# A decoder block's expert stage: which 128 tokens gather their experts, when, and which operand of the up product is stationary

## The chip, the cores and the metric

One core of one Trainium2 chip runs the whole layer in one launch. Its engines run their own instruction streams: TensorE (PE; weight loads PEld), VectorE (DVE), ScalarE (ACT), GpSimd (POOL) and SyncE (SP, used for DMA issue). The metric is the device time of one execution in microseconds; lower is better.

## The reference, cut to what matters

```python
h = rmsnorm(x, norm1_g);  z = h @ w_in                      # 512 tokens x 2048
a_out = chunked_spatial_gating(gelu(zu), gelu(zv), ...)
b_out = sliding_window_attention(zq, zk, zvv, sinks)
x = x + concatenate([a_out, b_out]) @ w_out
h2 = rmsnorm(x, norm2_g)
# peer(h2): 8 heads, 128 x 128 product keys, 16 experts of 16384 for each head and token
q = h2 @ w_query;  s1, s2 = q @ sub_keys
experts, gates = top16(top16(s1) + top16(s2)), softmax
a = gelu(h2 . expert_down[experts]);  x = x + sum(gates * a * expert_up[experts])
out = rmsnorm(x, norm_f_g)
```

## The kernel before

The 512 tokens are four blocks of 128. Every product is made of three matmuls in fp32r (`mm3`, L131 to L133): high part by high part, high by low, low by high. The weights come as chunks of 1 MiB (`wraw`, two buffers), loaded by SP in the order of use (L100). Each chunk is two pieces of 1024 columns; a piece is split by ACT into its high part (`whi`, L110) and by DVE or POOL into the rest (`wlo`, L112), into four buffers, two pieces ahead of PE. The load of chunk n+2 can start when both pieces of chunk n are split. `W.on_pool` is the list of pieces whose `wlo` POOL makes; from the thirteenth down chunk on it is always DVE.

The program is one long sequence:

- **A**, 26 chunks: norm, input projection, attention, spatial gating.
- **B**, 16 chunks: output projection of all four blocks (`project`, 512 columns of weights moving, the mixer's tokens `mxh`, `mxl` stationary; 24 matmuls for a piece), residual, second norm, turn to columns (`to_columns`).
- **C**, 16 chunks: queries. Blocks 0 to 2 ("dense") have the tokens moving, 384 columns; block 3 ("gathered", `GB`) has the weights moving. Behind each quarter come the scores, and `choose`, which is VectorE work (`best16`), is put into a `Filler` that a call `fill.tick(budget)` empties between matmuls.
- **D**, 51 down chunks: `dn` = 128 experts by 384 tokens, 48 matmuls, gelu, stored in `a_dram`. Between them run what is left of the choice, the decoding of it (`decode`), and a table of gates: 96 `quad`s of four tokens, each with one-hot rows `eq` (DVE, L719) and `p1` (DVE L726 or ACT), a product `p2` on POOL (L722), four matmuls of 256 columns (L738), and an evacuation by ACT (`low`) and DVE (`stage`, L754).
- **E and F**: 77 more down chunks and 128 up chunks. `up` has the dense tokens stationary and 512 columns of weights moving, three blocks, 4608 matmuls in all; each quarter is added by DVE to the tokens' rows `acc` (L978). Block 3 never meets the dense products: for each of its tokens 128 experts' rows (down, then up) are fetched by indirect DMA in halves of 1024 columns (`fetch`, L879, 512 of them, issued by POOL) and consumed by one VectorE instruction each (`unit`, L894 and L901), against `half_row` in PSUM. They are paced over this part alone.
- The last quarter of the last `up` runs block by block, with the final norm and the output behind each.

## Time and profile before

| | us |
|---|---|
| median of 3 runs (range) | 3049.59 (3042.21 to 3051.31) |
| profiled execution, span | 3046.2 |
| stage A, 0 to 388.9 | 388.9 |
| stage B, 388.9 to 582.0 | 193.1 |
| stage C, 582.0 to 786.5 | 204.5 |
| stage D, 786.5 to 1339.0 | 552.5 |
| stages E and F, 1339.0 to 3035.0 | 1696.0 |
| tail, 3035.0 to 3046.2 | 11.2 |

The profile gives no more of the profiled execution than its span; that lies inside the range of the runs, 3.4 us under their median. The stages are cut by hand at the first or last matmul of each. A row of the view of busy time by stretch has the stretch, its length, the busy time of PE, PEld, DVE, ACT and POOL with their instruction counts, the granted TensorE clock (1.00 is full), the busy share of the DMA engines and GB/s. In a timeline a row is start, length, engine, line, operation, output and input tile, form, count, and in brackets the idle time before it and what ended it. Matmuls overlap, so their spacing is read from their starts, not from their lengths. In a group of instructions the numbers behind the count are busy time, mean ns of one, and idle time of the engine just before them.

### The profile page before, as it was taken

What the parts mean: (1) busy time and instruction counts of PE and PEld (TensorE: products, weight loads), DVE (VectorE), ACT (ScalarE), POOL (GpSimd) and SP (SyncE); (2) the same over time, 40 slices, a digit from 0 to 9 for tenths busy, and PEclk for the clock granted to TensorE, in tenths of its full rate; (3) what the DMA queues carried; (4) which work ended last, traced back from release to release, by engine and by line L of the source; (5) the groups of instructions that cost most, each with busy time, mean ns of one, the idle gap of its engine ahead of it and who ended that gap; (6) DMA issues with size and microseconds to landing.
All of it is one profiled execution on the core that took longest, in us unless ns stands there. A gap on an engine that the chain in (4) does not pass through costs nothing.

```text
span 3046.2 us, 38888 instructions
## 1 busy us (share of the span) xinstructions
PE 2939.4 (96%) x15021; PEld 2623.7 (86%) x15021; DVE 2228.9 (73%) x3266; ACT 1095.9 (36%) x1699; POOL 1220.4 (40%) x754
## 2 busy tenths in 40 slices
PE   7999999999989888999999999999999999999998
PEld 6888878799989888898788889898998989899896
DVE  3125642359998999967888887878888888888864
ACT  3244432222236655643323233232322323232333
POOL 2132100334435555633344344545445454554522
PEclk9999999999999999999999999999999999999999
DMA  5221242322334444569888888998989898898953
GB/s 188 90 82 57 70 166 88 120 83 84 110 115 159 155 168 160 195 250 350 302 312 333 328 304 316 328 328 311 331 312 339 312 336 314 318 340 314 338 212 132
DMA packets 193866, 696.85 MB, mean 229 GB/s; under 512 B 16528, under 2 KB 81296, under 8 KB 148240
## 3 DMA queue, kind: packets, MB, share of 16 engines
q1 hardware_dynamic: 104960, 378.04, 35.0%
q0 software_dynamic: 73728, 268.47, 24.4%
q10 hardware_dynamic: 14992, 47.86, 4.0%
q8 instruction: 118, 1.93, 0.3%
q14 instruction: 68, 0.56, 0.1%
HBM read 650.78 MB, written 43.52 MB: 228 GB/s over the span
## 4 chain that ended last, share of the span: by engine, by line
PE 49%; DVE 20%; issue 15%; POOL 10%; ACT 3%; DMA 2%; ACTq 0%; POOLq 0%; SPq 0%; DVEq 0%
POOL row L879 10%; PE dn L133 5%; PE acc L131 5%; PE dn L132 5%; PE dn L131 5%; PE acc L133 5%; PE acc L132 5%; PE up L132 5%; PE up L131 5%; PE up L133 5%; DVE wlo L112 4%; DVE stage L754 3%; DVE eq L719 2%; DVE cand L572 1%; PE tr L339 1%
## 5 line engine op out<-in xcount | busy, mean ns | idle before, releaser
L110 ACT CAST whi<-wraw 128x1024 fp32r<-128x1024 f32 x628 | 639.7, 1048 | 738.9 <-DMA wraw<-in_up 321.1
L112 DVE TENSOR_TENSOR wlo<-wraw,whi 128x1024 fp32r<-128x1024 f32 x550 | 719.5, 1312 | 252.9 <-ACT whi L110 251.9
L133 PE MATMUL dn<-h2d,wlo 128*128 128x384 f32 x2048 | 695.2, 339 | 28.8 <-DVE wlo L112 25.6
L131 PE MATMUL dn<-h2d,whi 128*128 128x384 f32 x2048 | 694.0, 339 | 8.4 <-ACT whi L110 8.4
L132 PE MATMUL dn<-h2d,whi 128*128 128x384 f32 x2048 | 692.3, 338 | 0.0
L131 PE MATMUL up<-whi,gah 128*128 128x512 f32 x1536 | 598.9, 390 | 3.2 <-DVE acc L978 3.0
L132 PE MATMUL up<-wlo,gah 128*128 128x512 f32 x1536 | 598.8, 390 | 3.0 <-DVE wlo L112 3.0
L133 PE MATMUL up<-whi,gal 128*128 128x512 f32 x1536 | 598.3, 390 | 0.0
L879 POOL DMA_INDIRECT row<-in_down_rows,idx x256 | 367.6, 1436 | 492.0 <-DVE row L894 470.2
L879 POOL DMA_INDIRECT row<-in_up_rows,idx x256 | 364.7, 1425 | 366.4 <-DVE half_row L901 345.5
L133 PEld LDWEIGHTS dn<-h2d,wlo 128*128 128x128 f32 x2048 | 388.1, 190 | 37.3 <-DVE wlo L112 33.1
L112 POOL TENSOR_TENSOR wlo<-wraw,whi 128x1024 fp32r<-128x1024 f32 x78 | 194.9, 2519 | 559.0 <-ACT whi L110 559.0
L131 PEld LDWEIGHTS dn<-h2d,whi 128*128 128x128 f32 x2048 | 388.5, 190 | 10.5 <-ACT whi L110 10.1
L132 PEld LDWEIGHTS dn<-h2d,whi 128*128 128x128 f32 x2048 | 388.4, 190 | 0.4
L131 PEld LDWEIGHTS up<-whi,gah 128*128 128x128 f32 x1536 | 288.8, 188 | 65.9 <-DVE acc L978 4.7
L132 PEld LDWEIGHTS up<-wlo,gah 128*128 128x128 f32 x1536 | 288.6, 188 | 63.3 <-DVE wlo L112 4.4
L133 PEld LDWEIGHTS up<-whi,gal 128*128 128x128 f32 x1536 | 288.8, 188 | 60.0
L901 DVE SCALAR_TENSOR_TENSOR half_row<-row,wgt,half_row 128x1024 f32<-128x1024 f32 x256 | 328.9, 1285 | 14.8 <-DMA row<-in_up_rows,idx 11.7
L894 DVE SCALAR_TENSOR_TENSOR row<-row,half_row 128x1024 f32<-128x1024 f32 x256 | 307.1, 1215 | 18.9 <-DMA row<-in_down_rows,idx 17.3
L722 POOL TENSOR_TENSOR p<-eq,gT 128x1024 fp32r<-128x1024 bf16 x96 | 236.2, 2468 | 206.9 <-DVE eq L719 196.0
L978 DVE TENSOR_TENSOR acc<-up,acc 128x512 f32<-128x512 f32 x192 | 129.3, 690 | 92.5 <-PE up L133 92.3
L951 ACT ACTIVATE aa<-dn 128x384 f32<-128x384 f32 x72 | 35.4, 492 | 348.2 <-PE dn L133 348.2
(194 smaller groups left out, 3441.6 us busy)
## 6 DMA issues: line engine op xcount, KB each, us to landing
wraw<-in_down SPq DMA_DIRECT2D x128, 1024.0 KB
wraw<-in_up SPq DMA_DIRECT2D x128, 1024.0 KB
wraw<-in_win SPq DMA_DIRECT2D x26, 1024.0 KB
g_dram<-stage ACTq DMA_DIRECT2D x24, 1024.0 KB
g<-g_dram SPq DMA_DIRECT2D x32, 768.0 KB
wraw<-in_wout SPq DMA_DIRECT2D x16, 1024.0 KB
wraw<-in_wq SPq DMA_DIRECT2D x16, 1024.0 KB
aa<-a_dram SPq DMA_DIRECT2D x56, 192.0 KB
```

Of the source, the lines that this page charges most:

```text
L110: self.nc.scalar.copy(hi, src)
L112: eng.tensor_sub(lo, src, hi.bitcast(F32))
L131: nc.tensor.matmul(ps, wh, xh, start=start, stop=False)
L132: nc.tensor.matmul(ps, wh, xl, start=False, stop=False)
L133: nc.tensor.matmul(ps, wl, xh, start=False, stop=stop)
L719: nc.vector.tensor_tensor(eq, iota[:, None, :].to_broadcast([P, 4, P]), t[:, 1, four, None].to_broadcast([P, 4, P]), op=OP.is_equal)
L722: nc.gpsimd.tensor_tensor(p2, eq[:, :, None, :].to_broadcast([P, 4, 2, P]), hl[:, four, :, None].to_broadcast([P, 4, 2, P]), op=OP.mult)
L754: nc.vector.tensor_tensor(stage[h][:, :, o:o + 4], ps[:, :, 0, k].rearrange("p t k -> p k t"), low[:, :, k].rearrange("p t k -> p k t"), o ...
L879: nc.gpsimd.indirect_dma_start(out=t, out_offset=None, in_=src, in_offset=bass.IndirectOffsetOnAxis(ap=idx[:, j, h:h + 1], axis=0))
L894: nc.vector.scalar_tensor_tensor(t, t, 1.0, half, op0=OP.mult, op1=OP.mult, accum_out=dots[:, j, h:h + 1])
L901: nc.vector.scalar_tensor_tensor(half, t, wgt[:, j:j + 1], half, op0=OP.mult, op1=OP.add)
L978: nc.vector.tensor_add(y, ps[b], y)
```

## The change

Block 0 takes the place of block 3 as the gathered block, and its part is done first. After the mixer, block 0 alone runs through the output projection (16 chunks), two chunks of the others' projection, and its queries (16 chunks); then the others' projection (14 chunks) and queries (16). `w_out` and `w_query` are so loaded and split twice: 32 chunks more. The gathered work of block 0 (512 units) is queued as soon as its choice is decoded, and is now issued from `mm3` by a rate (`Flow`) from the others' projection on. The last 32 tokens of block 3 leave the dense products too (`EX`), so these have 352 columns in place of 384: their 128 experts each are gathered as 4 groups of 32 on the 128 partitions, 128 units more. `up` has the weights stationary and the 352 tokens moving, 6144 matmuls, and adds into `accT` (columns); at the end the result is turned back to rows (`rows_out`). POOL makes a third to three quarters of the `wlo` in every stage after A. In the tables the two parts of a gate are added in PSUM by a second matmul, and the evacuation is ACT's alone; 88 quads. `half_row` has its PSUM from the output projection on.

```diff
-    chunks += [a["wout"][i] for i in range(16)]
-    chunks += [a["wq"][i] for i in range(16)]
+    chunks = [a["win"][i] for i in range(26)] + wout + wout[:2] + wq + wout[2:] + wq
...
-    W.on_pool = [range(0, 4), range(20, 36), range(2 * 42 - 2, 2 * 70)]
+    LEAD, REST, ASK, EXPERTS = 52, 52 + 68, 52 + 96, 52 + 128
+    def on_pool(p):
+        if p < LEAD:
+            return p < 4 or 20 <= p < 36
+        if p < REST:
+            return p % 3 == 2
+        if p < ASK:
+            return p % 2 == 0
+        if p < EXPERTS + 2 * OPEN:
+            return p % 4 != 0 if p < EXPERTS else p % 2 == 0
+        return p % 3 == 0
...
+class Flow:
+    def step(self, ns):
+        if not self.q:
+            return
+        self.credit = min(self.credit + ns * self.rate, 3.0)
+        while self.q and self.credit >= 1.0:
+            self.credit -= 1.0
+            self.q.popleft()()
...
     def mm3(ps, w, x, start, stop):
...
+        flow.step(3 * ps.shape[-1] * COL_NS)
...
+    for q in range(4):
+        ps = acc_tile()
+        for i in range(8):
+            project(ps, 0, i, W.get())
+        residual(ps, 0, q)
...
+    for g in range(4):
+        ps = row_tile()
+        for i in range(8):
+            hi, lo = W.get()
+            for k in range(2):
...
+                mm3(ps, (hT0[0][:, kt, :], hT0[1][:, kt, :]), (hi[:, c], lo[:, c]),
+                    kt == 0, kt == KT - 1)
+            if soon and i % 2:
+                soon.popleft()()
+            fill.tick(2.0)
...
+        residual(ps[b - 1], b, 3)
+        dst = second_norm(b)
+        turned = (dst, h2d, (b - 1) * P)
...
+    to_columns(*turned)
...
                 def products():
-                    ps = pst2.tile([P, 4, 2, P], F32, name="tr", bufs=3)
+                    ps = pst2.tile([P, 4, P], F32, name="tr", bufs=4)
                     for j in range(4):
-                        nc.tensor.matmul(ps[:, j].rearrange("p a k -> p (a k)"), p1[:, j, :],
-                                         p2[:, j].rearrange("p a k -> p (a k)"),
-                                         start=True, stop=True)
+                        for i in range(2):
+                            nc.tensor.matmul(ps[:, j], p1[:, j, :], p2[:, j, i, :],
+                                             start=i == 0, stop=i == 1)
...
-                    nc.scalar.copy(low, ps[:, :, 1, :])
...
-                        nc.vector.tensor_tensor(stage[h][:, :, o:o + 4],
...
+                        nc.scalar.copy(stage[h][:, :, o:o + 4],
+                                       ps[:, :, k].rearrange("p t k -> p k t"))
...
-            fill.tick(2.7)
+        fill.tick(2.4)
...
+            ps = [late["ps"].tile([P, TD], F32, name="up", bufs=4) for _ in range(4)]
+            def multiply(m, j, w):
+                k = (j % 2) * 512 + m * P
+                x = ga[CB * c + j]
+                mm3(ps[m], (w[0][:, k:k + P], w[1][:, k:k + P]), x, j == 0, j == CB - 1)
...
+            w = [W.get(1), W.get(2)]
+            for m in range(4):
+                for j in range(4, 8):
+                    multiply(m, j, w[j // 2 - 2])
+                y = accT[:, 4 * q + m, :]
...
+                    nc.vector.tensor_add(y, ps[m], y)
...
+    def rows_out(q):
+        for b in range(ND):
...
+            for m in range(4):
+                nc.tensor.transpose(ps[:n, m * P:(m + 1) * P],
+                                    late["acc"][:, 4 * q + m, b * P:b * P + n], ident)
+            y = late["x"][b]
+            nc.vector.tensor_add(y[:n, cols], ps[:n], y[:n, cols])
+            square(b, n, y, q, nc.vector if q == 3 else nc.gpsimd)
+            if q == 3:
+                last_norm(b, n, y, o_rows[b + 1][:n])
...
+    flow.rate = 1.0 / 4800.0
     for kind, i in order:
...
         down(i)
         if i == OPEN - 1:
-            while fill.q or ready:
+            while fill.q or fill.later or ready:
                 fill.tick(1e9)
                 take()
             open_late()
+            pace()
```

How the instructions stand, at three places. First DVE in the output projection: `wlo` is a split piece, `x` the residual of a block's quarter. Before, 8 pieces stand between the residuals of four blocks:

```order
193 L112 TENSOR_TENSOR wlo<-wraw,whi 128x1024 x8
194 L503 TENSOR_TENSOR x_2860<-acc,x_2860 128x512
195 L503 TENSOR_TENSOR x_2861<-acc,x_2861 128x512
196 L503 TENSOR_TENSOR x_2862<-acc,x_2862 128x512
197 L503 TENSOR_TENSOR x_2863<-acc,x_2863 128x512
```

And after, in the output projection of block 0 (the other pieces are POOL's):

```order
192 L120 TENSOR_TENSOR wlo<-wraw,whi 128x1024 x5
193 L549 TENSOR_TENSOR x_2883<-acc,x_2883 128x512
194 L120 TENSOR_TENSOR wlo<-wraw,whi 128x1024 x6
195 L549 TENSOR_TENSOR x_2883<-acc,x_2883 128x512
196 L554 TENSOR_REDUCE sst<-ss_2887 128x1
197 L556 SCALAR_TENSOR_TENSOR xn<-x_2883,rstd,gb_2885 128x2048
```

A quarter of the projection's weights now serves one block, so 8 pieces pass for 48 matmuls where they passed for 192.

Second POOL near the end of stage D (`p` is the table's product p2, `row` an indirect fetch). Before, it has the table's products alone there:

```order
106 L722 TENSOR_TENSOR p_9204<-eq,gT 128x1024
107 L722 TENSOR_TENSOR p_9261<-eq,gT 128x1024
108 L722 TENSOR_TENSOR p_9271<-eq,gT 128x1024
109 L722 TENSOR_TENSOR p_9310<-eq,gT 128x1024
110 L722 TENSOR_TENSOR p_9363<-eq,gT 128x1024
```

And after:

```order
286 L120 TENSOR_TENSOR wlo<-wraw,whi 128x1024
287 L682 DMA row<-in_down_rows,idx_2872 128x1024
288 L901 TENSOR_TENSOR p_11082<-eq,gT 128x1024
289 L682 DMA row<-in_down_rows,idx_2872 128x1024
290 L901 TENSOR_TENSOR p_11135<-eq,gT 128x1024
291 L901 TENSOR_TENSOR p_11145<-eq,gT 128x1024
292 L120 TENSOR_TENSOR wlo<-wraw,whi 128x1024
293 L901 TENSOR_TENSOR p_11191<-eq,gT 128x1024
294 L682 DMA row<-in_down_rows,idx_2872 128x1024
295 L901 TENSOR_TENSOR p_11248<-eq,gT 128x1024
```

Half of the split pieces and the fetches now stand between the products, and the last 22 products (295 to 316) stand in one row with nothing between them; on PE the matmuls of the last 25 quads stand in one row behind the 51st down chunk, where before none were left over.

Third PE in `up`. Before:

```order
5922 L133 MATMUL up<-whi,gal 128x512
5923 L131 MATMUL up<-whi,gah 128x512
5924 L132 MATMUL up<-wlo,gah 128x512
5925 L133 MATMUL up<-whi,gal 128x512
5926 L131 MATMUL up<-whi,gah 128x512
```

And after:

```order
5909 L144 MATMUL up<-gah,whi 128x352
5910 L145 MATMUL up<-gal,whi 128x352
5911 L146 MATMUL up<-gah,wlo 128x352
5912 L144 MATMUL up<-gah,whi 128x352
5913 L145 MATMUL up<-gal,whi 128x352
```

The moving operand is written first: 512 columns of weights before, 352 tokens after.

## Rows read from the trace of the kernel before

**Rows 1.** The page: busy time, share of the span and instructions, PE.
```profile
PE 2939.4 (96%) x15021; PEld 2623.7 (86%) x15021; DVE 2228.9 (73%) x3266; ACT 1095.9 (36%) x1699; POOL 1220.4 (40%) x754
```
**Rows 2.** Busy time by stretch: stages B, C, D, E with F, tail.
```profile
388.90:582.00 193.10, 186.31 (x820) 149.13 (x819) 71.35 (x82) 56.53 (x89) 7.15 (x9) 1.00 0.34 126
582.00:786.50 204.50, 198.77 (x1119) 188.30 (x1120) 144.22 (x566) 57.52 (x78) 84.50 (x36) 0.99 0.26 88
786.50:1339.00 552.50, 499.06 (x2853) 481.85 (x2852) 510.77 (x730) 302.62 (x585) 290.62 (x118) 0.97 0.45 156
1339.00:3035.00 1696.00, 1689.12 (x8297) 1504.38 (x8295) 1350.78 (x1638) 526.84 (x653) 748.93 (x527) 1.00 0.86 312
3035.00:3046.20 11.20, 0.00 (x0) 0.00 (x0) 2.17 (x4) 1.87 (x3) 0.74 (x2) 0.68 0.40 162
```
**Rows 3.** Timelines of PE: pairs of starts 42, 63 and 54 matmuls apart.
```profile
23.35 0.28 PE L132 MATMUL acc<-hT,whi 128*128 128x256 f32 x1
...
28.32 0.28 PE L132 MATMUL acc<-hT,whi 128*128 128x256 f32 x1
...
2699.72 0.34 PE L131 MATMUL dn<-h2d,whi 128*128 128x384 f32 x1
...
2710.64 0.39 PE L131 MATMUL up<-whi,gah 128*128 128x512 f32 x1
...
2722.88 0.39 PE L131 MATMUL up<-whi,gah 128*128 128x512 f32 x1
```
**Rows 4.** Timelines of PE, short forms: scores (128 columns), a quad's products (256).
```profile
639.03 2.84 PE L588 MATMUL tr<-subk,qd 128*128 128x128 f32 x24
...
925.35 0.63 PE L738 MATMUL tr<-p,p 128*128 128x256 f32 x4
```
**Rows 5.** Groups of instructions, whole span: a piece's split on ACT and on POOL.
```profile
L110 ACT CAST whi<-wraw 128x1024 fp32r<-128x1024 f32 x628 | 639.7, 1048 | 738.9 <-DMA wraw<-in_up 321.1 <-PE acc L133 168.9 <-PE up L133 102.6
...
L112 POOL TENSOR_TENSOR wlo<-wraw,whi 128x1024 fp32r<-128x1024 f32 x78 | 194.9, 2519 | 559.0 <-ACT whi L110 559.0
```
**Rows 6.** Timelines of DVE and SP in stage B, then half microseconds of busy time.
```profile
438.85 2.36 DVE L112 TENSOR_TENSOR wlo<-wraw,whi 128x1024 fp32r<-128x1024 f32 x2 [1.78 <-ACT whi L110]
...
441.24 0.33 SPq L100 DMA_DIRECT2D wraw<-in_wout  x1
...
442.00:442.50 0.50, 0.50 (x4) 0.39 (x3) 0.00 (x0) 0.50 (x1) 0.00 (x0) 1.00 1.37 213
...
445.00:445.50 0.50, 0.50 (x3) 0.38 (x3) 0.00 (x0) 0.00 (x0) 0.00 (x0) 1.00 0.59 246
```
**Rows 7.** Timeline at the end of stage B: residual to columns of the last block.
```profile
581.67 0.69 DVE L503 TENSOR_TENSOR x<-acc,x 128x512 f32<-128x512 f32 x1
...
597.29 0.69 DVE L208 TENSOR_TENSOR h2gT<-tr,h2gT 128x512 fp32r<-128x512 f32 x1 [0.17 <-ACT h2gT L207]
```
**Rows 8.** Groups of instructions in stage D alone (786.5 to 1339), DVE and POOL.
```profile
L112 DVE TENSOR_TENSOR wlo<-wraw,whi 128x1024 fp32r<-128x1024 f32 x80 | 141.3, 1766 | 28.1 <-ACT whi L110 27.7
L754 DVE TENSOR_TENSOR stage<-tr,low 128x256 f32<-128x256 f32 x192 | 107.8, 607 | 3.9 <-ACT low L751 3.9
L719 DVE TENSOR_TENSOR eq<-iota,eT 128x512 bf16<-128x512 f32 x96 | 94.9, 998 | 0.0
...
L722 POOL TENSOR_TENSOR p<-eq,gT 128x1024 fp32r<-128x1024 bf16 x96 | 236.2, 2468 | 206.9 <-DVE eq L719 196.0 <-PE tr L738 7.8 <-PE tr L702 3.2
L112 POOL TENSOR_TENSOR wlo<-wraw,whi 128x1024 fp32r<-128x1024 f32 x22 | 54.5, 2501 | 60.5 <-ACT whi L110 60.5
```
**Rows 9.** Busy time of the `wlo` tile's instructions alone, stages E with F.
```profile
1339.00:3035.00 1696.00, 1012.05 (x2766) 519.68 (x2765) 500.07 (x408) 0.00 (x0) 1.00 0.86 312
```
**Rows 10.** Groups of instructions, whole span: a unit's fetch and its VectorE instruction.
```profile
L879 POOL DMA_INDIRECT row<-in_down_rows,idx x256 | 367.6, 1436 | 492.0 <-DVE row L894 470.2 <-issue 19.7 <-DVE aa L860 2.2
...
L894 DVE SCALAR_TENSOR_TENSOR row<-row,half_row 128x1024 f32<-128x1024 f32 x256 | 307.1, 1215 | 18.9 <-DMA row<-in_down_rows,idx 17.3 <-ACT half_row L892 1.4
```
**Rows 11.** Two microseconds of busy time in stage D, behind 5 us without matmuls.
```profile
906.00:908.00 2.00, 1.79 (x6) 1.79 (x7) 1.47 (x6) 1.59 (x3) 0.00 (x0) 0.50 0.00 0
```

More of the change, by code (lines that the diff above doesn't have):

```diff
@@ L42 @@
 BIG = 3.0e38
+COL_NS = 0.4505
+MORE_ROWS = 4
 class Filler:
@@ new lines, in block_kernel, with fetch_to @@
+    fetched = 0
+    late = {}
+    def fetch_to(n):
+        nonlocal fetched
+        while fetched < min(n, len(units)):
+            i, src, h, j = units[fetched]
+            if "p" in late and fetched % (4 + MORE_ROWS) >= 4:
+                t = late["p"].tile([P, D // 2], F32, name="more", bufs=MORE_ROWS)
+            else:
+                t = pg.tile([P, D // 2], F32, name="row", bufs=4)
+            nc.gpsimd.indirect_dma_start(
+                out=t, out_offset=None, in_=src,
+                in_offset=bass.IndirectOffsetOnAxis(ap=idx[i][:, j, h:h + 1], axis=0))
+            rows_at[fetched] = t
+            fetched += 1
@@ new lines, in block_kernel @@
+    pq = tc.alloc_tile_pool(name="pq", bufs=1, reuse_waits="tile")
+    flow.rate = 1.0 / 5200.0
+    pending = None
+    for g in range(4):
+        cols = [*(acc_tile() for _ in range(3)), row_tile()]
+        for i in range(8):
+            hi, lo = W.get()
+            for k in range(2):
+                kt = 2 * i + k
+                for c in range(4):
+                    w = slice(k * 512 + c * P, k * 512 + (c + 1) * P)
+                    mm3(cols[c][:, :TL], (hi[:, w], lo[:, w]), (h2d[0][:, kt, :], h2d[1][:, kt, :]),
+                        kt == 0, kt == KT - 1)
+            if i == 0 and pending is not None:
+                pending()
+            fill.tick(3.6)
+        qd = pq.tile([P, 4, TL], F32, name="qd")
+        for c in range(4):
+            nc.scalar.copy(qd[:, c, :], cols[c][:, :TL])
+        pending = score_group(g, qd)
@@ L1006, in up @@
                             a_load(nxt + 7)
-                tick(weight(c, q))
-    o_rows = out.rearrange("(b p) d -> b p d", p=P)
+                tick()
+            if last and q:
+                rows_out(q - 1)
+            if nxt is not None and q == 3:
+                for j in range(4, 6):
+                    make_ga(nxt + j)
+            w = [W.get(1), W.get(2)]
[3 more added lines that the diff above has]
+                y = accT[:, 4 * q + m, :]
+                if c == 0:
+                    nc.scalar.copy(y, ps[m])
+                else:
+                    nc.vector.tensor_add(y, ps[m], y)
+            if nxt is not None and q == 3:
+                for j in range(6, 8):
+                    make_ga(nxt + j)
+            tick()
+            tick()
+        if last:
+            rows_out(3)
+        for j in range(CB):
+            del ga[CB * c + j]
     def open_last():
@@ L1032, in gathered_norm @@
-    def gathered_norm():
-        y = acc[GB]
-        for q in range(4):
-            cols = slice(q * 512, (q + 1) * 512)
-            nc.scalar.activation(late["junk"], y[:, cols], AF.Square,
-                                 accum_out=late["ss"][:, GB, q:q + 1])
-            nc.vector.tensor_mul(y[:, cols], y[:, cols], late["gf"][:, cols])
-        last_norm(GB)
-    def start_gather():
-        nonlocal pace
-        left = sum(2 for k, i in order if k == "d" and i >= NPRE)
-        left += sum(4 * weight(c, q) for c in range(NCHUNK) for q in range(4))
-        pace = len(units) / (left - 24.0)
-        for u in range(len(units)):
-            fill.paced.append(unit(u))
+        nc.vector.tensor_reduce(sf[:n], late["ss"][:n, b, :], axis=AX.X, op=OP.add)
@@ L1049, in block_kernel, with pace @@
+    def pace():
+        left = sum(2 * 24 for k, i in order if k == "d" and i >= OPEN)
+        left += sum(384 for k, i in order if k == "u")
+        flow.rate = len(flow.q) / (left * TD * COL_NS - 40e3)
+    flow.rate = 1.0 / 4800.0
     for kind, i in order:
```

639 lines of the change are left out of this document (338 added, 301 removed).

## The prediction, made before the changed kernel had run

> **What bounds the kernel now.** I read first the shares of the page [rows 1]: PE is busy for 96% of the span. Then the busy time by stage [rows 2], because that share hides two kinds of stage. In E with F, PE is busy for 1689 of 1696 us and the time is the number of matmuls by their pace. In D, VectorE is busy for 511 of 552.5 us and PE only for 499, so there a change has to take work from VectorE. B and C are PE stages with small holes.
>
> The pace comes from the starts in the timeline [rows 3]: 42 matmuls of 256 columns take 4.97 us, 118 ns each; 63 of 384 columns 10.92 us, 173.3 ns; 54 of 512 columns 12.24 us, 226.7 ns. That is 13.3 ns and 0.4167 ns for a column, and the 256-column row lies on it, so the weight load does not set the pace down to there. At 352 columns I take 160.0 ns. No row shows 352; its neighbours bound it to 118 and 173.3. At 128 columns it does not hold: 24 take 2.84 us [rows 4], (2.84 - 0.28) / 23 = 111 ns each.
>
> With this, E with F is 77 x 48 x 0.1733 = 641 us of down and 4608 x 0.2267 = 1044 us of up, 1685 of the 1696: its stalls are 11 us. The bound of the prediction is stage by stage; stage A does not change.
>
> **Stages E and F.** Now 77 x 48 x 0.160 = 591 us and 6144 x 0.160 = 983 us, together 1574, 111 less. Its cover: VectorE was busy for 1351 us. It loses 137 of the 410 split pieces to POOL, at 500 / 408 = 1.23 us [rows 9] 168 us; units are 640 less the 136 that the new order places ahead of E, 504 in place of 512; so about 1175 us of 1595, 74%. POOL gets 504 fetches by 1.44 us [rows 10] and 137 pieces by 2.5 us [rows 5], 1070 us, 67%. The traffic was 312 GB/s by 1696 us, 529 MB [rows 2]; about the same bytes in 1595 us are 330 GB/s. The new queue has no slower rate in the last quarter of an early `up`, where six gate products (make_ga, two VectorE instructions of 352 columns each) fall together: there VectorE has some 19 us of work for 15.4 us of PE (five units 6.8, three pieces 3.3, four adds 2, and 6.6 for make_ga, an estimate at half of the 1.2 us that 1024 columns take [rows 9, 10]). That lag can cost 0 to 20 us over six chunks; I take 10. Stalls 21, stage 1595: **-101 us**.
>
> **Stages B and C: block 0 alone.** The matmuls stay in number, but 32 chunks are loaded and split a second time, and 32 chunks now serve one block: 12 matmuls of 512 columns, 2.72 us of PE for a chunk where it was 10.9 or 11.0. Can a chunk be had in 2.72 us? In B, the second `wlo` ends at 441.2, SP issues the next load at 441.24, and its bytes move until 445.5 [rows 6]: 4.25 us. Then two casts of 1.05 on ACT and the last `wlo`: 1.2 us on VectorE [rows 6] or 2.5 on POOL [rows 5]; with a third of the pieces on POOL the split is 3.4 to 4.6, mean 3.8. Two buffers, so two chunks in 8.1 us: 4.1 us a chunk. Bounds: 2.72 (PE alone, if loads overlapped better) and 5.1 (if VectorE's queue delays each split by 2 us). In the projection the first two loaded chunks run at PE's pace but behind the mixer's own casts, which used to hide under four blocks and now leave PE about 10 us idle: 13.5 + 5.5 + 13 x 4.3 = 75 us, against 43.5 of PE. The queries have three chunks of lead, then choice work between the splits: 8 + 13 x 4.8 = 71. Between them two chunks for three blocks, 16, hide block 0's norm; its transposes add 4.
>
> The rest of the projection is 28 pieces by 18 x 0.2267 = 4.08, 114 us, plus 12 for transposes, for a cold load queue that also fetches 3 MB of x, and for VectorE's decoding: 126. Then the new exposure: all dense queries need the last block's columns, while before this block's turn was covered by the other blocks' matmuls. That chain takes 581.7 to 598.0, 16.3 us [rows 7]; one POOL piece fewer stands in it: 14. Queries of three blocks: 32 x 24 x 0.1733 = 133, scores 8, and VectorE, which has 13 choices and 25 units there, lags a little: 150. Sum 75 + 20 + 71 + 126 + 14 + 150 = 456 against 397.6: **+58 us**, between +15 and +100.
>
> **Stage D.** PE: 51 x 48 x 0.160 = 392, and the table's products go from 384 of 256 columns at (0.63 - 0.28) / 3 = 117 ns [rows 4], 45 us, to 704 of 128 columns at 111 ns, 78. So 475 in all, as before: the 33 us won on down are given back. VectorE: 511, less 29 pieces by 1.77, less the 108 us of `stage`, less 8 `eq` [rows 8], less one of four decodings (some 20), plus 11 more one-hots (10), plus 80 units by 1.3 [rows 10], 104: about 437. POOL had 291 us and gets 88 products by 2.47, 51 pieces by 2.5 [rows 8] and 82 fetches by 1.44 [rows 10]: 463. So the bound of 511 falls to three engines at 437 to 475. ACT takes `stage` in place of `low`; the price of its strided copy is not in the trace, from 0.4 to the 0.6 that VectorE needed [rows 8], for 176 of them 70 to 106 us, and ACT had 303 of 552 us. But the order puts the last 22 POOL products in a row behind the 51st down chunk: 22 x 2.3 = 50 us in which PE has 20 us of short matmuls. Before that, 455 us of PE by the old ratio of time to bound, 552.5 / 511 = 1.08: 491. Stage D 545: **-7 us**, between -45 and +40.
>
> The two readings of POOL and VectorE in rows 8 and 9 matter here: a `wlo` on VectorE takes 1.77 us in D, where POOL computes, and 1.23 in F, where it only issues fetches. By the Trainium skill, SBUF — State Buffer, section "Who interferes with whom", a VectorE instruction with two SBUF inputs and a GpSimd instruction that reads SBUF exclude each other for their whole length; the trace agrees, and by that rule POOL's new pieces in F would lengthen VectorE's there.
>
> **Tail.** Before, the last quarter of `up` ended block by block and one block's chain remained (VectorE 2.2, ACT 0.8 ahead of it, POOL 0.7 [rows 2]: about 4 us and the output). Now three blocks follow the last matmul one after another: 11.2 + 2 x 4 + 1: **+9 us**.
>
> **Sum.** 58 - 7 - 101 + 9 = -41 us on the span of 3046.2. The median of the runs lies 3.4 above this span: 3049.6 - 41 = **3009 us**. A change under 0.3% (9 us) can't be told from none.
>
> **Rivals.**
> 1. *The loads keep up and D is freed.* If transfers overlap so that block 0's chunks run at PE's 2.72 us, 26 x 1.5 = 39 us are saved, and if D is set by PE's 475 and 31 of the last products, another 39: 2931 with both, 2970 with one. For it: VectorE's bound in D does fall. Against it: 4.25 us in rows 6 is one load on an idle queue. Chance 0.2.
> 2. *POOL and VectorE in turn (slower).* POOL computes for 343 us in F where it computed for none, a fifth of the stage; 520 VectorE instructions with two SBUF inputs would wait 0.54 x 0.2 / 0.5 = 0.2 us each, 110 us, mostly hidden at 74%, but not in the early `up` chunks, where 19 us for 15.4 become 21: 6 x 5.5 = 33 in place of 10, and as much again in the quarters beside them. In D POOL's computing rises from 291 to 345 us: 25 to 40 us. 3009 + 45 + 35 = 3089. It decides where VectorE in the first `up` chunks is busy for over 95%. Chance 0.2.
> 3. *The clock.* Behind 5 us without matmuls the granted clock is 0.50, the 1.2 GHz level [rows 11]. If block 0's gaps of 1.4 us bring that, its chunks take 5.44 us on PE: 26 x 1.3 = 34, so 3043: no change that can be told. Against: block 0's PE would still be busy for two thirds, and a busy PE got its clock back behind that row. By the Trainium skill, TensorE: Matmul & The Clock Gate, section "HAM oscillation", a loop whose bursts are shorter than its wait for DMA is throttled again in each pass, which is this shape. No run here shows it with gaps this short. Chance 0.1.
> 4. *The traffic is at its limit.* If F gets no more than its 312 GB/s, 520 MB take 1667 us, +72: 3081, slower; half of it 3045. For it: the DMA engines are busy for 86%. Against: so they have 14% left. Chance 0.08.
>
> My forecast, 2980 to 3040, has 0.42.
>
> **Range and chances.** Faster than 3040.4: the forecast but for 0.02 at its upper edge, and rival 1: 0.60. Within 0.3%: rival 3, half of rival 4, that edge: 0.16. Slower than 3058.7: rival 2, half of 4: 0.24. Range 2945 to 3080: it leaves out the far half of rival 1 and the upper half of rival 2.
>
> **What would show it.** Down and up matmuls 160 ns apart; 4.1 us for a chunk of block 0 with the casts waiting for DMA; some 14 us without matmuls ahead of the dense queries; 50 us of POOL products in a row at the end of D with PE half idle; E with F near 1595 us. It is wrong if 352 columns don't pace at 160 ns, if block 0's stages take under 130 us or over 190, or if VectorE stalls PE in the early `up` chunks.

## The result, and the profile after

The changed kernel takes 3169.97 us (median, 3169.0 to 3170.06) where the kernel before took 3047.88 on the same chip: a ratio of 1.0405 [1.039, 1.042], **slower by 122 us**. The forecast was 3009, and its range ended at 3080. The profiled execution has a span of 3168.0 us, against 3005 by the sum: 163 us are to be found.

The page of after, busy time and share of the span (as [rows 1] of before): PE has more instructions and is busy for less, 92% where it was 96%.

```profile
PE 2908.4 (92%) x16925; PEld 2748.2 (87%) x16925; DVE 2318.6 (73%) x3218; ACT 1133.9 (36%) x1776; POOL 1672.8 (53%) x1071
```

Busy time by stretch of after, to be laid beside [rows 2] (stretch, length; busy PE, PEld, DVE, ACT, POOL with their instructions; granted clock, DMA share, GB/s). The first three rows are parts of the front: block 0's projection, block 0's queries, the rest of the projection with the chain behind it. The fourth is the dense queries; then the whole front, the last part of stage D, all of D, E with F, the last `up` alone, the tail.

```profile
389.50:473.40 83.90, 58.06 (x203) 40.49 (x202) 45.79 (x46) 41.19 (x53) 29.50 (x10) 0.90 0.59 217
...
491.40:572.60 81.20, 60.86 (x230) 43.58 (x228) 64.69 (x142) 37.53 (x43) 27.97 (x11) 0.89 0.55 200
572.60:738.30 165.70, 137.93 (x566) 107.43 (x565) 121.23 (x207) 46.97 (x69) 80.11 (x54) 0.91 0.67 246
738.30:886.30 148.00, 145.57 (x866) 144.52 (x865) 116.72 (x361) 47.42 (x61) 82.82 (x49) 1.00 0.57 199
...
389.50:886.30 496.80, 419.45 (x1939) 349.64 (x1938) 356.62 (x761) 179.22 (x233) 226.44 (x127) 0.93 0.61 218
...
1391.50:1457.30 65.80, 46.84 (x201) 42.57 (x199) 61.89 (x37) 34.94 (x104) 57.11 (x27) 0.52 0.32 123
...
886.30:1457.30 571.00, 518.26 (x3165) 507.97 (x3163) 547.22 (x711) 269.77 (x565) 435.95 (x221) 0.91 0.63 225
1457.30:3145.90 1688.60, 1601.42 (x9879) 1587.87 (x9879) 1259.39 (x1485) 528.86 (x675) 917.39 (x653) 0.98 0.83 311
...
3026.30:3145.90 119.60, 71.39 (x424) 69.82 (x424) 57.08 (x59) 30.43 (x53) 33.06 (x23) 0.79 0.38 138
3145.90:3168.00 22.10, 1.74 (x13) 1.01 (x10) 6.94 (x13) 5.62 (x9) 2.21 (x6) 0.65 0.36 130
```

Beside the forecast, in us of the span:

| stage | before | forecast | after | miss |
|---|---|---|---|---|
| front (B, C) | 397.6 | 456 | 496.8 | +41 |
| D | 552.5 | 545 | 571.0 | +26 |
| E with F | 1696 | 1595 | 1688.6 | +94 |
| tail | 11.2 | 20 | 22.1 | +2 |

The largest miss is in the stage whose arithmetic was surest. Its pace holds: 100 us of stage F, where PE had no idle time and 628 instructions:

```profile
2200.00:2300.00 100.00, 100.00 (x628) 100.00 (x627) 79.85 (x79) 34.46 (x44) 57.66 (x41) 1.00 0.86 322
```

That is 159.2 ns for a matmul of 352 columns (160.0 forecast). So 9840 of them are 1567 us, and 122 of the 1688.6 are beyond that. About half stand in the last `up`: 119.6 us for 384 matmuls, which are 61.1. PE's waits there (engine, line, tile, what it waited for: us in total, times, longest):

```profile
PE up L144 <- ACT whi L118: 24.5, 1, 24.5
PE dn L1187 <- DVE xr L1190: 22.2, 3, 21.5
```

Who held the cast back, in the timelines of SP, VectorE and ScalarE in the same stretch (start, length, instruction, in brackets the idle time before it and what ended it), and four us of busy time between:

```profile
3026.63 2.54 SPq L1158 DMA_DIRECT2D xr<-x_dram  x3
...
3029.78 0.53 SPq L1199 DMA_DIRECT2D xf<-x_dram  x1
...
3047.19 2.29 DVE L1200 TENSOR_TENSOR yf<-yf,xf 128x2048 f32<-128x2048 f32 x1 [18.45 <-DMA xf<-x_dram]
...
3049.52 0.63 ACT L1177 ACTIVATE junk<-yf 128x512 bf16<-128x512 f32 x1 [21.34 <-DVE yf L1200]
...
3056.21 1.15 ACT L1172 ACTIVATE yf<-yf,rstd 128x1024 f32<-128x1024 f32 x1 [3.70 <-POOL rstd L1168]
3057.77 3.89 ACT L118 CAST whi<-wraw 128x1024 fp32r<-128x1024 f32 x4 [0.42 <-ACT yf L1172]
```
```profile
3036.00:3040.00 4.00, 0.00 (x0) 0.00 (x0) 0.00 (x0) 0.00 (x0) 0.00 (x0) 0.56 1.01 424
```

Read from below: the casts of the next weights start at 3057.8, since ScalarE works through the squares and the scaling of block 0's rows first. Those wait for VectorE's add at 3047.2, and that for the load of `xf` issued at 3029.8, 17 us before, behind three loads of x and one of y. From 3036 to 3044 the bytes move at 424 GB/s and no engine computes. `finish_first` puts the add into VectorE's stream in the same breath as its loads, and what stands behind it in that stream waits with it.

PE's second wait, 21.5 us up to 3101.7, is of the same kind. The add into `xr` that the transposes wait for stands on VectorE behind the sums of the last 32 tokens (`finish_last`), which wait 7.4 us for their load and then run for 9.8:

```profile
3087.01 9.82 DVE L1215 TENSOR_TENSOR xf<-xf,more 32x1024 f32<-32x1024 f32 x8 [7.43 <-DMA xf<-x_dram]
```

### The profile page after: what moved, and what is told of

It reads as the page before. It is cut to its first block, busy times and chain, and to the rows that moved or that the text cites. A ratio compares the mean times of both kernels' runs of the same rounds, so it can differ in the third digit from the quotient of the medians.

```text
span 3168.0 us, 43607 instructions
## 1 busy us (share of the span) xinstructions
PE 2908.4 (92%) x16925; PEld 2748.2 (87%) x16925; DVE 2318.6 (73%) x3218; ACT 1133.9 (36%) x1776; POOL 1672.8 (53%) x1071
## 5 line engine op out<-in xcount | busy, mean ns | idle before, releaser
L120 POOL TENSOR_TENSOR wlo<-wraw,whi 128x1024 fp32r<-128x1024 f32 x269 | 684.3, 2546 | 923.4 <-ACT whi L118 818.5
L144 PE MATMUL up<-gah,whi 128*128 128x352 f32 x2048 | 668.7, 327 | 48.2 <-ACT whi L118 32.9
L146 PE MATMUL dn<-h2d,wlo 128*128 128x352 f32 x2048 | 670.2, 327 | 36.3 <-POOL wlo L120 25.6
L146 PE MATMUL up<-gah,wlo 128*128 128x352 f32 x2048 | 664.2, 324 | 11.2 <-POOL wlo L120 6.1
L145 PE MATMUL dn<-h2d,whi 128*128 128x352 f32 x2048 | 668.8, 327 | 0.0
L144 PE MATMUL dn<-h2d,whi 128*128 128x352 f32 x2048 | 665.4, 325 | 3.0 <-ACT whi L118 3.0
L145 PE MATMUL up<-gal,whi 128*128 128x352 f32 x2048 | 662.8, 324 | 0.0
L144 PEld LDWEIGHTS up<-gah,whi 128*128 128x128 f32 x2048 | 388.5, 190 | 56.1 <-ACT whi L118 34.0
L146 PEld LDWEIGHTS up<-gah,wlo 128*128 128x128 f32 x2048 | 388.3, 190 | 15.2 <-POOL wlo L120 8.1
L145 PEld LDWEIGHTS up<-gal,whi 128*128 128x128 f32 x2048 | 389.4, 190 | 0.0
L708 DVE SCALAR_TENSOR_TENSOR half_row<-more,wgt,half_row 128x1024 f32<-128x1024 f32 x160 | 205.2, 1282 | 1.4
```

Source lines behind the costliest of these rows:

```text
L120: eng.tensor_sub(lo, src, hi.bitcast(F32))
L144: nc.tensor.matmul(ps, wh, xh, start=start, stop=False)
L145: nc.tensor.matmul(ps, wh, xl, start=False, stop=False)
L146: nc.tensor.matmul(ps, wl, xh, start=False, stop=stop)
L708: nc.vector.scalar_tensor_tensor(half_row, t, wgt[i][:, j:j + 1], half_row, op0=OP.mult, op1=OP.add)
```

## The experiments

Medians are given with the ratio to the kernel before on the same chip (3040 to 3044 us there); after stands at 1.0405. Stage by stage the profiled executions are compared. One stage, block 0's queries, differed by about 8 us between kernels with the same code there, so less than that in one stage isn't read as an effect.

**1. The finish in the last `up`, later.** In `finish_first`, the add, the squares and the scaling go into the streams four steps of the loop behind the loads (at a quarter's end); the last 32 tokens' rows in three steps.

```
         nc.sync.dma_start(x, x_dram[0])
-        nc.vector.tensor_add(y, y, x)  ...
+        waiting.append((tick_no + 4, rest))
```

> The arithmetic of the finished rows of block 0 and of the last 32 tokens is put further back in the program: their loads stay where they are, but the add, squares and scaling of block 0 come one quarter of the last up later, and the adds of the last 32 tokens are spread over seven of its steps. Theory (in-order queues): in the changed kernel VectorE and ScalarE stand 18.5 and 21.3 us behind a load of x that has only just been issued, so the casts of the next weights stand too; PE is idle from 3034 to 3058 and again from 3080 to 3101 and runs at 1.2 GHz for 7 us behind the first hole. Then the run is 40 to 55 us under the changed kernel's 3168 (3113 to 3128), and the stretch behind the last down product falls from 120 us to some 75. Rival (the loads of 5 MB take the place of weights whatever the order): the holes stay at 15 us or more each, gain under 20 us.

3157.6 us, 1.0378 [1.0348, 1.0408]. From the last down matmul to the end 119.9 us instead of 141.7. The add still waits for its load, and ScalarE still stands behind it:

```profile
3055.95 2.29 DVE L1205 TENSOR_TENSOR yf<-yf,xf 128x2048 f32<-128x2048 f32 x1 [6.14 <-DMA xf<-x_dram]
3058.27 0.63 ACT L1180 ACTIVATE junk<-yf 128x512 bf16<-128x512 f32 x1 [15.73 <-DVE yf L1205]
```

The mechanism is touched and not removed: 22 us in that stretch and 12 in the medians, less than the theory wanted.

**2. The same in more steps.** The add eight steps behind, the scaling eleven; the last 32 tokens are added in place.

```
+            after(later, scaled)
...
+        after(8, rest)
```

> The finished rows of block 0 and the last 32 tokens are handled in steps, each placed a quarter or more behind the load that it needs: block 0's add and squares at the eighth step behind the last down product, its scaling at the eleventh; the last 32 tokens in place in the rows of block 3, the adds at 4 and 7 steps behind their loads, the scaling at 10. Theory (in-order queues): the stretch from the last down product to the end, 142 us in the changed kernel and 120 with the adds one quarter later, falls to 90 to 105: 61 of up, 7 of transposes, 22 of tail. Rival (the 5 MB loaded there keep the weights waiting): not under 115.

3152.9 us, 1.0365 [1.0323, 1.0406]; last down to end 118.0 us, no better, as the rival had it (not under 115). Now VectorE and ScalarE are free, and the weights themselves are late: the first cast waits for its load, which stands with 5 MB of x and y in the transfers (timeline of ScalarE).

```profile
3054.96 1.05 ACT L118 CAST whi<-wraw 128x1024 fp32r<-128x1024 f32 x1 [16.30 <-DMA wraw<-in_up]
```

So the stall has two layers: a queue held by a wait, and behind it a burst of loads placed together.

**3. Loads and work both spread.** Each block's x is loaded one step after the other from ScalarE's queue, block 0's y and x six and seven steps on, the work at step eleven; and in the change of groups (below) the second group's rows are fetched eight tokens earlier, since the first group's result no longer shares their buffer.

```
+                if j == n - 8 and h == 1 and i + 1 < len(counts):
+                    stage_in(i + 1, 0)
...
-            nc.sync.dma_start(t, x_dram[b + 1])
+            after(1 + b, lambda b=b, t=t: nc.scalar.dma_start(t, x_dram[b + 1]))
```

> The changed kernel, block 0 still alone and first, with only the two waits of the last part taken out as in the one-pass run with the new finish. Theory (these waits and the second pass over the weights are separate costs): the one-pass run fell from 3054 to 3008 by them, 46 us; here they give 35 to 50, 3168 to 3118 to 3133, all of it behind 2640 us; ahead of that nothing moves. Rival (part of that gain came with the one pass, whose E and F were fuller): under 25 us.

3134.1 us, 1.0308 [1.0278, 1.0338], 36 us less than after: the theory's 35 to 50, at its low end. E with F 1643.3 us (1467.9 to 3111.2) instead of 1688.6; E begins 10.6 us later, which I can't put down to the edit. The last `up` by busy time, and 100 us around the change of groups:

```profile
3026.30:3111.20 84.90, 69.70 (x424) 68.89 (x423) 58.89 (x58) 30.32 (x53) 38.24 (x23) 0.90 0.50 190
```
```profile
2600.00:2700.00 100.00, 100.00 (x627) 100.00 (x627) 78.26 (x93) 36.01 (x45) 58.38 (x43) 1.00 0.91 339
```

34.7 us less in the last `up`, where PE still waits 15 us for the rows `xr`; and 100.0 in place of 92.73 us of PE in the second stretch, where VectorE of the changed kernel had stood for 13 us:

```profile
2661.07 1.02 ACT L695 COPY half_row<-hst 128x1024 f32<-128x1024 f32 x1 [11.76 <-DMA hst<-h_dram]
2662.11 1.22 DVE L696 SCALAR_TENSOR_TENSOR row<-row,half_row 128x1024 f32<-128x1024 f32 x1 [13.21 <-ACT half_row L695]
```

**4. No early units.** The queue of gathered rows is not served during the front and D; all 640 units fall into E and F. Three rates become 0, of which one is shown.

```
-    flow.rate = 1.0 / 2600.0
+    flow.rate = 0.0
```

> The gathered rows are not consumed before E: the three rates ahead of it are set to zero, so all 640 units lie in E and F. Theory: 136 units cost VectorE 1.21 us each and stand in its queue ahead of residuals and splits while they wait for their rows; the rest of the projection falls from 166 us (572.6 to 738.3) to about 145, D from 572 to about 540 since VectorE and POOL are its bound; E with F takes 640 units by 1.25 us, VectorE at some 87% and traffic at some 360 GB/s, and gets 0 to 40 us longer. Sum -50 to -10 against 3168. Rival (the early units cost nothing, and traffic bounds E with F): front and D move by under 10 us and E with F grows by over 50 us, since 600 MB at its 316 GB/s need 1900 us.

3165.2 us, 1.0403 [1.0353, 1.0454]: no change. But the stages shift (rest of the projection, D, E with F by busy time):

```profile
579.90:727.10 147.20, 130.23 (x566) 102.97 (x565) 82.69 (x145) 46.05 (x68) 41.81 (x23) 0.96 0.44 164
872.60:1389.70 517.10, 497.43 (x3163) 491.66 (x3163) 470.10 (x516) 268.68 (x564) 346.20 (x140) 0.94 0.45 163
1389.70:3147.40 1757.70, 1633.76 (x9879) 1613.06 (x9879) 1398.89 (x1757) 530.79 (x677) 1063.92 (x789) 0.96 0.89 339
```

18.5 us less ahead of the dense queries and 54 less in D, as the theory said; 69 more in E with F, as the rival said; for 136 units moved. A unit costs about half a microsecond wherever it stands: the early start, which the forecast charged to D at 104 us of VectorE and then called covered, buys nothing and costs nothing.

**5. Half-size loads for the weights.** Four buffers of 512 KB instead of two of 1 MB, one load for each piece.

```
-            self.raw[i] = self.pool.tile([P, 2048], F32, name="wraw", bufs=2)
+            self.raw[p] = self.pool.tile([P, 1024], F32, name="wraw", bufs=4)
```

> The weights are loaded in halves of a chunk, 512 KB into four buffers instead of 1 MiB into two, so that a load can start as soon as one piece is split. Theory (the two chunk buffers set the 4.63 us for a chunk of block 0): with the next half already under way the projection and the queries of block 0 take 3.2 to 4.0 us for a chunk, 10 to 30 us less in the two stages together (they take 84 and 81 us), and nothing elsewhere: 3135 to 3160. Rival (the split by ScalarE, VectorE and POOL sets the pace, or the transfer itself): both stages stay within 5 us.

3159.6 us, 1.0385 [1.0329, 1.0440], not to be told from 1.0405. Block 0's queries begin at 485.8 instead of 491.4; a chunk of its projection takes 4.3 us instead of 4.6, by the starts of the matmuls from the fourth chunk on.

**6. And no low part on POOL in block 0's stages.** As 5, with the pieces that POOL split in block 0's projection and queries given to VectorE.

```
         if p < REST:
-            return p % 3 == 2
+            return False
```

> The changed kernel with loads in halves of a chunk, and in block 0's projection and queries all low parts on VectorE (1.2 us each) in place of every third on POOL (2.4 us). Theory (a chunk of block 0 waits in turn for its load, the cast and the low part; the halves took 4.63 to some 4.2 us for a chunk): with the short low part 3.3 to 3.8 us for a chunk in the projection, 84 to about 68 us from its start to the norm; in the queries, where VectorE also has the choice, under 5 us of change against the 78 of the run with halves. Rival (the transfers set the pace): the projection stays within 4 us of the run with halves.

3159.8 us, 1.0392 [1.0362, 1.0423]. The queries begin at 480.5, 10.9 us sooner; a chunk of the projection takes 3.9 us. The stretch up to the queries, and what ScalarE waited for (389 to 481):

```profile
389.50:480.50 91.00, 72.09 (x279) 51.71 (x278) 60.64 (x63) 47.79 (x61) 0.75 (x2) 0.94 0.72 245
```
```profile
ACT whi L118 <- DMA wraw<-in_wout: 22.1, 19, 5.8
```

Of the 0.7 us less for a chunk, the halves alone gave 0.3 (run 5) and the split on VectorE 0.4. With POOL idle and the buffers halved, what ScalarE still waits for is transfers, 22 us of 91. That comes close to the theory's 3.3 to 3.8 us a chunk; the transfers alone don't set the pace.

**7. One pass, most of the change kept.** All four blocks are projected and asked together, as in the kernel before; 352 tokens dense, weights stationary in `up`, units and finish as in after. The edit also gives POOL the pieces that it had before up to D, so there it splits 23 in place of 51.

```
-    chunks = [...] + wout + wout[:2] + wq + wout[2:] + wq
+    chunks = [...] + wout + wq
```

> The part of the change that runs block 0 alone is undone: output projection and queries of all four blocks in one pass over the weights as in the kernel before, with 32 chunks fewer to load and split, low parts on POOL as there up to D; the rest stays (32 tokens gathered, weights stationary in up, tables). The gathered units start in D, behind block 0's decoding. Theory (the second pass costs what the stages show): from 389 to the first down product 400 us in place of 497; D 520 to 570; E with F takes some 600 units in place of 504 and loses part of that, 1700 to 1760 in place of 1688: 3060 to 3130. Rival (running block 0 ahead pays for itself, since 136 units are out of E and F): 3150 or more.

3055.8 us, 1.0040 [1.0020, 1.0059]: 114 us less than after, somewhat more than the theory gave. Front, D, E with F up to the last `up`, and the last `up`:

```profile
389.00:786.60 397.60, 385.08 (x1938) 337.44 (x1938) 215.55 (x647) 113.94 (x166) 91.60 (x44) 1.00 0.30 112
786.60:1323.70 537.10, 498.26 (x3164) 488.90 (x3162) 515.19 (x673) 270.17 (x567) 360.96 (x179) 0.95 0.62 224
1323.70:2910.60 1586.90, 1536.38 (x9458) 1523.01 (x9458) 1274.36 (x1566) 500.17 (x623) 958.40 (x699) 0.99 0.90 343
2910.60:3031.80 121.20, 71.63 (x424) 69.13 (x423) 56.21 (x62) 30.30 (x53) 35.07 (x26) 0.79 0.41 152
```

The front is back at the 397.6 of before, 99 less than after; D 34 less, with fewer units and fewer of POOL's pieces in it (run 8); E with F 1708.1, 19.5 more, with the units that come later. Running block 0 ahead costs some 100 to 114 us net: up to 13 of the 114 can be POOL's pieces in D.

**8. D: low parts back to VectorE.** The pieces that POOL split in D.

```
-            return p % 4 != 0 if p < EXPERTS else p % 2 == 0
+            return p % 4 != 0 if p < EXPERTS else False
```

> In D all 102 low parts of the weights are made by VectorE instead of every second one by POOL. Theory (VectorE and POOL exclude each other over long stretches there: VectorE's own low parts take 2.72 us behind POOL's and 1.23 us where POOL is quiet): POOL's 51 pieces hold both engines for 51 x 2.4 = 122 us and VectorE's would take 51 x 1.2 = 61, so D gets 20 to 60 us shorter than its 572 and the mean low part on VectorE falls under 2.2 us. Rival (VectorE is simply short of time, busy for 97% from 1061 to 1392, and POOL relieves it): 51 x 1.23 = 63 us more VectorE work make D 30 to 70 us longer.

3155.4 us, 1.0371 [1.0341, 1.0401]. D is 13.5 us shorter with 53 more instructions on VectorE. The stage by busy time, and the low parts on VectorE from 1056 to its end (line, operation, tile, count | busy, mean ns):

```profile
882.50:1440.00 557.50, 512.59 (x3164) 501.82 (x3162) 543.90 (x764) 269.70 (x566) 318.08 (x171) 0.92 0.64 230
```
```profile
L120 DVE TENSOR_TENSOR wlo<-wraw,whi 128x1024 fp32r<-128x1024 f32 x63 | 120.3, 1910 | 2.2 <-ACT whi L118 2.2
```

The changed kernel, D from 1061 to its end, one-hots, low parts and POOL's low parts:

```profile
L905 DVE TENSOR_TENSOR p<-iota,eT 128x512 fp32r<-128x512 f32 x43 | 90.9, 2115 | 0.0
L120 DVE TENSOR_TENSOR wlo<-wraw,whi 128x1024 fp32r<-128x1024 f32 x30 | 82.4, 2745 | 4.7 <-ACT whi L118 4.7
L120 POOL TENSOR_TENSOR wlo<-wraw,whi 128x1024 fp32r<-128x1024 f32 x30 | 81.5, 2716 | 0.7 <-ACT whi L118 0.5
```

Twice as many low parts on VectorE take 1.91 us each instead of 2.75: VectorE's busy time falls by 3 us. More than half of what counted as a low part's time on VectorE was waiting for POOL ([rows 9] have 1.23 us for one without it). The direction is the theory's, the size is below its 20 us.

**9. The table's products sooner.** The work between the down chunks of D is served faster, so that less is left for the end.

```
-        fill.tick(2.4)
+        fill.tick(3.4)
```

> The changed kernel with a budget of 3.4 in place of 2.4 for the work put between the down products, so that the table's products are all issued before the 51st down product and none are left in a row behind it. Theory (VectorE and POOL, who take turns, bound the stage from the first table product on): the row of 23 products behind the last of the 51 (66 us) goes, but the down products get later by as much; from the first down product to the end of the tables 571 us changes by under 15. Rival (the row at the end is an avoidable loss, since PE does 20 us of work in 66): 30 to 45 us less.

3208.5 us, 1.0552 [1.0531, 1.0573], slower than after by some 40 us. D is 610.2 us:

```profile
889.40:1499.60 610.20, 525.32 (x3166) 509.50 (x3165) 561.31 (x711) 271.00 (x568) 427.21 (x221) 0.92 0.59 211
```

The table ends at 1432.5 instead of 1457, but the low parts now stand behind more filler in the streams of VectorE and POOL: PE waits 67 us for them (34 in after), and the eight downs left over run afterwards, 67 us with PE always busy and VectorE for 36. Neither theory gave this. So the row at the end of D can't be taken out this way, and the work of VectorE and POOL alone doesn't set D: the order counts too.

**10. F: low parts back to VectorE.** POOL splits nothing behind D.

```
-        return p % 3 == 0
+        return False
```

> In E and F all low parts of the weights are made by VectorE, none of the 136 by POOL. Theory (VectorE and POOL exclude each other): VectorE's low parts there fall from 1.48 us to about 1.25, so that 136 more of them cost it 167 less 68 = 99 us in 1688, and POOL is quiet but for its fetches; PE's waits for low parts (24 us in E and F) shrink and the stretch gets 5 to 30 us shorter. Rival (VectorE's share of time is what counts: 77% becomes 83%): PE waits longer for the sums into accT and the stretch gets 10 to 40 us longer.

3165.7 us, 1.0407 [1.0376, 1.0437]: no change, E with F 1686.4 us. A low part on VectorE takes 1.227 us there (408 of them), the 1.23 of [rows 9], and in after 1.481 (272, with POOL's 136 beside them): the group of this run, then of after.

```profile
L120 DVE TENSOR_TENSOR wlo<-wraw,whi 128x1024 fp32r<-128x1024 f32 x408 | 497.8, 1227 | 130.5 <-ACT whi L118 129.3 <-issue 0.7 <-PE up L146 0.4
```
```profile
L120 DVE TENSOR_TENSOR wlo<-wraw,whi 128x1024 fp32r<-128x1024 f32 x272 | 402.2, 1481 | 140.5 <-ACT whi L118 139.0 <-PE up L146 1.4
```

So POOL does lengthen VectorE's instructions in F, by a quarter of a microsecond, and it costs the stage nothing: neither the theory's 5 to 30 us less nor the rival's 10 to 40 more.

**11. Units by quarter.** The rate falls to 0.4 in the last quarter of an early `up` and rises elsewhere.

```
-        self.credit = min(self.credit + ns * self.rate, 3.0)
+        self.credit = min(self.credit + ns * self.rate * self.weight, 3.0)
```

> The gathered units of E and F run at 0.4 of their rate in the last quarter of an up whose next gate products are still to be made, at 0.85 in its other quarters and at 1 behind, as the kernel before had it (0.4, 0.9 and 1). Theory (VectorE lags where six gate products, five units and the sums fall together): PE's waits for sums into accT, 15 us, and some of those for low parts between 1504 and 2000 go, the stretch is 10 to 25 us shorter. Rival (the holes come from the weights' loads and the splits): under 5 us.

3168.8 us, 1.0417 [1.0385, 1.0449]: no change, E with F 1683.4. PE's waits for the sums into `accT` ahead of the last `up` stay too, 13.9 us for 15.2: the units' rate doesn't set them.

**12. One pass with the finish spread.** 7 and 3 together.

> One pass over the weights for all four blocks, as in the run of that name, and two waits of the last part taken out: the rows that the finish needs are loaded one at a time from ScalarE's queue in the last up (blocks 1 to 3 at steps 1 to 3, block 0 at 6 and 7), block 0 is added at step 11 and scaled at 14, the last 32 tokens are added at 5 and 8 steps behind their units and scaled at 10; and the second gathered group's first rows are loaded before the first group's result is written, which no longer shares their buffer. Theory (the holes of the last up and of the change of groups are waits of in-order queues): from the last down product to the end 143 us in the one-pass run, 90 to 110 here; the wait of 13 us at the change of groups gone; 3054 falls to 3005 to 3030, faster than the kernel before. Rival (the 5 MB and the small adds stay in the way wherever they are put): not under 3040.

3007.9 us, 0.9890 [0.9873, 0.9906]: 1.1% under the kernel before, and 5% under after. Front 397.6, then D, E with F up to the last `up`, and the last `up`:

```profile
786.10:1320.80 534.70, 495.81 (x3164) 485.88 (x3163) 514.78 (x673) 270.18 (x567) 361.31 (x179) 0.96 0.62 225
1320.80:2894.20 1573.40, 1536.67 (x9457) 1523.76 (x9458) 1276.11 (x1566) 500.05 (x623) 962.75 (x699) 0.99 0.91 346
2894.20:2985.90 91.70, 70.13 (x424) 69.06 (x422) 59.26 (x61) 30.21 (x53) 39.20 (x26) 0.87 0.53 197
```

E with F is 1665.1 us. That it comes to the forecast's 3009 is chance: its front is 58 us shorter than forecast, its E with F 70 longer.

## Why the prediction was wrong, point by point

**Right.** The pace (159.2 for 160.0 ns) and so 1567 for 1574 us of pure work; that loads and splits bound block 0's two stages, 165 us and inside the 130 to 190 that the text allowed, though 146 was the sum; the exposed chain, 12 us (726 to 738) for 14; the dense queries, 148 for 150; that a row of POOL products ends D, though not its length; the tail, +11 for +9.

**Wrong: "Stalls 21, stage 1595".** They are 122, and the stage 94 us longer. I priced the one lag that I looked for, and left unpriced what the diff puts at the end: two finishes whose arithmetic enters in-order streams right behind its own loads. The text counted a moved step's matmuls and vector work, not its waits, and not what is queued behind the waiting instruction. Runs 1 to 3 show it: 35 us of the last `up` and some 7 to 11 at the change of groups go when loads and work are spread, 45 of the 94 in E with F. Of the 64 us ahead of the last `up`, PE's waits in the trace make up 39: 15 for VectorE's sums into `accT`, 12 for low parts, 11 for casts, the two largest being:

```profile
PE up L144 <- DVE accT L1135: 15.2, 17, 2.4
PE up L144 <- ACT whi L118: 8.4, 3, 5.8
```

The forecast's 10 for the early `up` is of the size of the first. Runs 10 and 11 leave it at 15.5 and 13.9, so neither POOL's pieces nor the units' rate sets it; what does stays open. In the other 25 us PE isn't idle but short of its pace, and the starts of its matmuls divide them: 67 matmuls at a granted clock of 0.50 (the 1.2 GHz level), at the start of E and behind some of the waits, come 314 ns apart, 10 us; the 9349 at full clock come 160.1 ns apart on average, 8 us over 159.2; and the last matmul ahead of each of 33 waits takes 0.32 us to end, where the next would have started after 0.16, 6 us.

**Wrong: "+58" in the front; it is +99.** Block 0's two stages took 19 us more than their sum, 165 for 146. A chunk of its projection took 4.6 us, not 4.1 to 4.3: waiting for a whole chunk is 0.3 of it (run 5), POOL's splits are 0.4 (run 6). In the queries, 81 us for 71, run 6 changed too little to say what the ten are; that stays open. More is in "the rest of the projection ... 126" and its chain of 14: 166 in place of 140. The text put 12 us for transposes, a cold load queue and decoding together, and placed early units into VectorE's stream without asking what stands behind them. They wait for their gathered rows, 28.6 us in eight waits, with residuals and low parts of the projection behind (timeline of VectorE in that stretch):

```profile
631.79 1.22 DVE L696 SCALAR_TENSOR_TENSOR row<-row,half_row 128x1024 f32<-128x1024 f32 x1 [6.20 <-DMA row<-in_down_rows,idx]
```

Without the units it took 147 (run 4). Rival 3, the clock, came on top in places: three times in block 0's projection PE falls to 1.2 GHz (granted clock 0.50). By the starts and ends of the matmuls it falls at 398.0, behind a gap of 2.9 us; at 421.9, behind gaps of 1.7 and 1.9 us with 0.5 us of matmuls between; and at 449.2, in the second of two gaps of 1.6 and 2.0 us with 0.5 between. Single gaps of 1.6 to 2.2 us there brought no fall.

```profile
398.00:401.00 3.00, 0.63 (x1) 0.12 (x1) 3.00 (x6) 2.68 (x3) 1.19 (x1) 0.50 0.14 57
...
422.00:425.00 3.00, 3.00 (x9) 2.34 (x8) 1.76 (x2) 1.59 (x2) 1.28 (x1) 0.50 0.43 126
```

But over the stage the clock is 0.90: it falls in three of the sixteen passes, not in each. By the Trainium skill, TensorE: Matmul & The Clock Gate, section "HAM oscillation", a loop whose bursts are shorter than its wait for DMA is throttled again in every pass. The prediction called block 0's loop of this shape, but by its own figures it isn't: 2.7 us of matmuls for a chunk against gaps of 1.4, and 1.9 as measured (4.6 less 2.7). So block 0's stages don't put the rule to the test.

**Wrong: "-7" in D; it is +18.5.** The sum took VectorE's 437 and POOL's 463 us as work side by side. In part they exclude each other: at the end of D, VectorE and POOL take turns (timelines of both; 5.2 us for two quads, and a one-hot of 512 columns takes 0.68 us alone, 2.38 beside a product).

```profile
1397.90 0.68 DVE L905 TENSOR_TENSOR p<-iota,eT 128x512 fp32r<-128x512 f32 x1
...
1401.84 2.38 DVE L905 TENSOR_TENSOR p<-iota,eT 128x512 fp32r<-128x512 f32 x1
1404.14 2.98 DVE L898 TENSOR_TENSOR eq<-iota,eT 128x512 bf16<-128x512 f32 x2
```
```profile
1401.46 4.52 POOL L901 TENSOR_TENSOR p<-eq,gT 128x1024 fp32r<-128x1024 bf16 x2 [0.70 <-DVE eq L898]
1406.66 4.52 POOL L901 TENSOR_TENSOR p<-eq,gT 128x1024 fp32r<-128x1024 bf16 x2 [0.69 <-DVE eq L898]
```

So the row of products at the end, put at 22 x 2.3 = 50 us, took 65.8, 16 of the 26 us that the forecast missed (PE is busy for 46.8 of them, at a granted clock of 0.52); the text's own 491 and 50 are 541, not its 545. VectorE was busy for 547 us where 437 was the sum; without any unit (run 4) for 470, where the sum less its 104 of units is 333. The text had the rows for this ([rows 8] and [rows 9], 1.77 against 1.23) and the rule beside them (the Trainium skill, SBUF — State Buffer, section "Who interferes with whom"), and used it for F alone, where run 10 shows it to be hidden. In D, where the rule agrees with the trace, it became a rival at 0.2 instead of a term. With VectorE's 547 as bound, the text's own 1.08 would have given 591, and 571 was measured. Run 8 bears the mechanism out in kind: without POOL's 51 pieces D is 13.5 us shorter.

**The rivals.** Rival 1 fell: the loads did not overlap better, and D was not freed. Rival 2 was right in D and wrong in F (run 10: real, but hidden); its 3089 is still 81 us short, since it has neither the waits at the end nor the front's. Rival 3 occurred as an addition of a few passes. Rival 4 fell: stretches of run 7 and 12 move 343 and 346 GB/s in E and F.

**The second pass.** Run 7 gives the plain answer: what the change spends on running block 0 ahead is 99 us of the front, some 18 of them for units served there (run 4) and the rest for loading and splitting 32 chunks twice and for the chain that is no longer covered. The early start that it buys is worth nothing (run 4).

## What to carry to other kernels

Price a moved step by its waits: for each instruction that needs a load issued just ahead of it, name what stands behind it on its in-order engine, and put it into the stream only when the load has had time; when that is mended, look at the burst of loads next. Before moving elementwise work from VectorE to POOL, compare one instruction's mean time beside a busy POOL and beside an idle one: where they differ, price it at the mean beside the busy POOL, since neither engine's sum alone is the bound. (To add the two sums would overshoot: 437 and 463 are 900 us, and D took 571.) Starting work early is worth something only if it costs less there than in its old place: here 136 units cost 72 us ahead of E and 69 in E and F.

## What the runs showed of the hardware that was not expected

A load of 1 MB placed behind four others landed 17 us after its issue, while the core moved up to 424 GB/s. The granted clock fell to 0.50 behind two gaps of 1.7 and 1.9 us with 0.5 us of matmuls between, and not behind single gaps of 1.6 to 2.2 us in the same stage. An elementwise instruction on VectorE took up to 3.5 times as long beside POOL's product (2.38 for 0.68 us). Filling PE's gaps more densely with table work made the kernel slower by some 40 us (run 9): PE waited 67 us in D for low parts that stand behind it in the streams, where it had waited 34.
